# Four seven-product couples in both mixers' output projections, their weight sums made ahead by way of HBM, and an affine step moved from VectorE to ScalarE

## The chip, the cores and the metric

The kernel runs on one core of a Trainium2 chip. The metric is the device time of one execution in microseconds (us). TensorE (PE) multiplies matrices, VectorE (DVE) and ScalarE (ACT) do element-wise work, GpSimd (POOL) some more of it, and SyncE (SP) issues most of the DMA transfers between HBM and the on-chip memory.

## The reference

An encoder trunk of two layers over one sequence of 256 tokens, model width 2048. Layer 0 has a bidirectional mLSTM mixer (8 heads), layer 1 a bidirectional HGRN2 mixer (16 heads); each is followed by a ConvGLU feed-forward network (FFN, 5504 wide).

```python
def mlstm_mixer(hn, w_in, b_gate, head_g, w_out):
    p = hn @ w_in
    ...
    y = head_rmsnorm(y, head_g, A_HEADS) * jax.nn.sigmoid(o)
    return y @ w_out

def hgrn_mixer(hn, w_in, lb, head_g, w_out):
    p = hn @ w_in
    ...
    def gate(f):
        log_f = jnp.logaddexp(log_lb, log_1mlb + jax.nn.log_sigmoid(f))
        k = (1.0 - lb) * jax.nn.sigmoid(-f)
    ...
    y = head_rmsnorm(y, head_g, B_HEADS) * jax.nn.silu(g)
    return y @ w_out
```

`y @ w_out` is the output projection that the change is about, a product of 256 x 2048 by 2048 x 2048. The gate is, without logarithms, `g = lb + (1 - lb) * sigmoid(f)`: the affine step of the change.

## The kernel before, in words

Products are made in float32 precision out of three products of reduced ones: each operand is split into a high part (`wh`, a cast on ScalarE at L144) and a low part (`wl`, a subtract on VectorE at L145), both in `parts`. Raw weights come in tiles `raw` of 128 x 2048 (1 MB), three in rotation, loaded in order on SP's queue (`load_raw`, L132). So every weight passes through a DMA, ScalarE and VectorE before TensorE reads it.

A projection is a list of chunks, each of 512 output columns and both halves of 128 tokens. In `mixed`, which makes both mixers' output projections, column block 0 is an ordinary chunk (`c0`, matmuls at L356), columns 512 to 1535 are a couple (`two`, made by `pair`, matmuls at L231), and column block 3 is again an ordinary chunk (`c3`). A couple has 8 units, each of two 128-row blocks of the weights: a 2 x 2 product of blocks that takes eight products, each of three matmuls of 128 x 512. For the units listed in `SEVEN_MIX`, (2, 4, 6), a scheme with seven products is used instead (`squares_by_seven`): it needs sums of four token blocks (`token`, `token_sums`: tile f at L635 and L540, then the split sums sx at L541 and L542) and sums of the weights' blocks.

In the mixers' couples the weights' sums are made in place by `combine` (L203): four VectorE subtracts of 128 x 512 for each unit, into a tile T and into raw itself. The FFNs' couples do it otherwise: their sums were made ahead. `prepare` loads the unit's raw weights into two tiles praw (on SP's queue, through `late` at L378), makes the sums by four subtracts (L603), and stores them in HBM (`tscr`, L606); the couple then loads T (768 KB, L194) and the last quarter of raw (256 KB, L195) from `tscr`. `prepare` is a side job with a period that sets how often a unit is made; the first eight units of each layer's FFN are prepared in the mixer before it (`prepare_early`, called with a first time and a period: 45.0 and 19.0 in layer 0, 30.0 and 26.0 in layer 1), the others in the FFN.

T and the token-sum tile f have the same tag "avc" (`temporary`): three buffers in the FFN's pool "ff", two in the pool "op" of a mixer's couple. This pool is opened when c0 is done in program order and lies over the memory of the mixer's own pool, so its first tiles wait for the last readers of the mixer's tiles, among them the last transposes pz (L1087 in layer 1).

The order of instructions on each engine is made by a scheduler that models their times; loads on SP's queue wait there in order until the buffer that they write is free.

In `hgrn`, each head and direction makes the gate: Sigmoid of z on ScalarE (L978), Sigmoid of −z (L979), then the affine step on VectorE (L980), and GpSimd's product with q (L981), from which the chunked recurrence goes on.

Of the kernel before, what the change touches and what calls it, by code (L numbers as in the profile page):

```python
# [49 lines left out]
SEVEN = (1, 2, 3, 4, 6, 7, 8, 9), (1, 2, 4, 5, 7, 8)  # L50
SEVEN_END = (1, 2, 3, 4, 5, 6, 7)
END = 3
SCRATCH = 4096
SEVEN_MIX = (2, 4, 6)

# [7 lines left out]
def trunk_kernel(ctx, tc, xT, x_d, fg_d, pp_d, cst_d, w_gate, w_first, w_aq, w_ak, w_av, w_ao, w_aout, w_ao2,  # L63
                 w_bq, w_bv, w_bg, w_bout, w_bo2, w_up, w_d0, w_d1, w_d2, w_d3, out, mscr, tscr):
    nc = tc.nc
# [61 lines left out]
    pin = tc.keep_in_program_order  # L127
    turns = dict(w=0)

# [488 lines left out]

    def mixed(w, w2, x, norm, close):

        c0, _, _, c3 = project(lambda c: w[c // 3], KT, x, norm)
        op, SX, first = ExitStack(), {}, c0.done

        def sums(u):
            side.until(lambda: u in SX)
            return SX[u]

        two = pair(w2, KT, 1, x, sums, norm, SEVEN_MIX)

        def token():  # L630
            for i, u in enumerate(SEVEN_MIX):
                f = temporary(two.pool, "f")
                for j in range(2):
                    y = x(2 * u + j).bitcast(F32)
                    dve.tensor_tensor(f[:, j * T:(j + 1) * T], y[:, 0:T], y[:, T:2 * T], ALU.add)  # L635
# [12 lines left out]
        return [c0, two, c3]  # L648


    def mlstm(norm, nxt):
# [192 lines left out]
        for pr in range(AH // 2):  # L844
# [36 lines left out]
            def done_first(ps, done_v=done_v):  # L881
# [10 lines left out]
                side.push(start(gs))  # L892
                prepare_early(box["mp"], 0, 45.0, 19.0)

# [30 lines left out]

        return chunks + mixed(w_aout, w_ao2, yx, nxt, stack.close)


    def hgrn(norm, nxt):
# [4 lines left out]
        def begin():  # L934
            mp = box["mp"] = stack.enter_context(tc.tile_pool(name="hg", bufs=1))
            late(cst[:, C_LV:], cst_d[:, C_LV:])
            prepare_early(mp, 1, 30.0, 26.0)
            box["turn"] = 0
# [23 lines left out]
        def take(hd, what, ps):  # L962
# [16 lines left out]
            act.activation(kz, z, AF.Sigmoid, scale=-1.0)  # L979
            dve.tensor_scalar(g, g, oml[:, hd:hd + 1], lb[:, hd:hd + 1], ALU.mult, ALU.add)  # L980
            pool.tensor_tensor(QZ[:, (1 - dr) * T:(2 - dr) * T], st["q"], g, ALU.mult)  # L981
# [143 lines left out]

        return chunks + mixed(w_bout, w_bo2, yx, nxt, stack.close)


    def ffn(layer, norm, nxt):
        stack = ExitStack()  # L1130
        ending = isinstance(nxt, FinalNorm)
        seven = SEVEN[0], SEVEN_END if ending else SEVEN[1]
        box = dict(n=(2 * len(SEVEN[0]) + len(SEVEN[1])) * layer)
        chunks, pairs = [], []
# [41 lines left out]
        for part, (f0, nf) in enumerate(((0, FA), (FA, FB))):  # L1176
# [137 lines left out]
def build(nc, ins, out_shape=(2, P, D), **kw):  # L1314
# [3 lines left out]
    mscr = nc.dram_tensor("mscr", (64, T), F32, kind="Internal").ap()  # L1318
    tscr = nc.dram_tensor("tscr", (4 * len(SEVEN[0]) + len(SEVEN[1]) + 2 * len(SEVEN_END), P, 2048), F32, kind="Internal").ap()
    with tile.TileContext(nc, schedule_with_timeline_sim=True) as tc:  # L1320
# [17 lines left out]
```

## Time and profile before

| | us |
|---|---|
| median of 3 runs (2383.26 to 2383.58) | 2383.42 |
| profiled execution | 2384.87 |
| its span in the trace | 2382.9 |

| stretch of the profiled execution | from, us | to, us |
|---|---|---|
| layer 0's mixer up to its couple | 10 | 326 |
| layer 0's couple (a) | 326 | 368 |
| layer 1's mixer up to its couple | 1080 | 1577 |
| layer 1's output columns 0 to 511 | 1577 | 1608.4 |
| layer 1's couple (b) | 1608.4 | 1656.1 |

The profile gives for each engine how long it was busy, for each line of the kernel the number, busy time and mean duration of its instructions and the idle time before them with what ended it ("idle before <-releaser"). The chain of waits follows the work that ended last back from the end, and lists in order of time what the end depended on. A view by windows gives busy times, the granted TensorE clock (PEclk, 1.00 is full speed) and DMA traffic for a stretch. Matmuls follow each other faster than the duration shown for one, because they are pipelined; their pace is the distance of starts. Names are those of the program's tiles: `wl<-raw,wh` reads raw and wh and writes wl.

### The profile page before, as it was taken

How to read it: one execution, taken by the hardware profiler on the slowest of the kernel's cores; microseconds unless marked ns; L12 is line 12 of the kernel's file. 1: busy time of each engine (PE TensorE's matmuls, PEld its weight loads, DVE VectorE, ACT ScalarE, POOL GpSimd, SP SyncE). 2: the span in 40 equal slices, each digit the busy share in tenths (PEclk: the TensorE clock that was granted, in tenths of full speed). 3: DMA queues.
4: the chain of work that ended last, by engine and by line, in shares of the span. 5: the costliest groups of instructions: out<-in, count | busy, mean ns of one | idle time of the engine just before them, and what ended most of it. 6: DMA issues, size and time to landing. Idle time of an engine off the chain costs nothing.

```text
span 2382.9 us, 38182 instructions
## 1 busy us (share of the span) xinstructions
PE 2365.6 (99%) x14572; PEld 2024.3 (85%) x14572; DVE 1938.4 (81%) x3001; ACT 1433.6 (60%) x2271; POOL 205.4 (9%) x242
## 2 busy tenths in 40 slices
PE   9999999999999999999999999999999999999998
PEld 7888888888888888888888888887888888888886
DVE  7777687888788887766888888888788788888787
ACT  7655456555665555655666666665555566455565
POOL 0100000000000000001233222320000000000000
PEclk9999999999999999999999999999999999999999
DMA  8777656886697885755666666764788588887695
GB/s 300 240 272 268 227 174 214 302 303 226 223 354 272 283 280 195 274 190 204 244 234 228 246 236 227 245 225 173 258 299 283 195 309 310 288 288 253 204 345 201
DMA packets 112471, 601.23 MB, mean 252 GB/s; under 512 B 12688, under 2 KB 13200, under 8 KB 66464
## 3 DMA queue, kind: packets, MB, share of 16 engines
q1 hardware_dynamic: 110592, 594.78, 71.1%
q0 software_dynamic: 1120, 3.21, 0.8%
q8 instruction: 114, 1.87, 0.3%
q10 hardware_dynamic: 576, 0.79, 0.1%
q14 instruction: 69, 0.57, 0.1%
HBM read 542.05 MB, written 56.69 MB: 251 GB/s over the span
## 4 chain that ended last, share of the span: by engine, by line
PE 95%; DVE 2%; DMA 1%; issue 1%; ACT 0%; SPq 0%; POOL 0%; DVEq 0%; POOLq 0%; ACTq 0%
PE mm L340 36%; PE mm L356 18%; PE mm L344 18%; PE pc L231 12%; PE mm L231 6%; DMA praw<-in_w_d 1%; PE py L1066 1%; PE pn L808 1%; DVE wl L145 1%; PE pd L1016 0%; PE pz L417 0%; PE pa L1016 0%; DVE QK L1029 0%; DMA Mb<-mscr 0%; DMA raw<-in_w_first 0%
## 5 line engine op out<-in xcount | busy, mean ns | idle before, releaser
L340 PE MATMUL mm<-xt,wh 128*128 128x512 f32 x3776 | 1314.2, 394 | 0.0
L145 DVE TENSOR_TENSOR wl<-raw,wh 128x1024 fp32r<-128x1024 f32 (+1 forms) x845 | 1034.6, 1229 | 274.6 <-ACT wh L144 268.9
L144 ACT CAST wh<-raw 128x1024 fp32r<-128x1024 f32 (+1 forms) x845 | 875.6, 1042 | 520.4 <-PE mm L340 293.6
L344 PE MATMUL mm<-xt,wl 128*128 128x256 f32 x3776 | 1046.3, 278 | 0.0
L340 PEld LDWEIGHTS mm<-xt,wh 128*128 128x128 f32 x3776 | 706.2, 188 | 160.1
L344 PEld LDWEIGHTS mm<-xt,wl 128*128 128x128 f32 x3776 | 709.7, 188 | 4.5 <-issue 0.4
L356 PE MATMUL mm<-wh,xt 128*128 128x512 f32 x1024 | 320.5, 391 | 2.2 <-ACT xt L362 1.6
L231 PE MATMUL pc<-wh,g 128*128 128x512 f32 x676 | 228.0, 389 | 0.0
L356 PEld LDWEIGHTS mm<-wh,xt 128*128 128x128 f32 x1024 | 191.1, 188 | 41.8 <-ACT xt L362 2.0
L356 PE MATMUL mm<-wl,xt 128*128 128x512 f32 x512 | 197.9, 391 | 0.0
L603 DVE TENSOR_TENSOR praw<-praw 128x512 f32<-128x512 f32 x208 | 143.8, 691 | 49.4 <-DMA praw<-in_w_d 39.0
L231 PEld LDWEIGHTS pc<-wh,g 128*128 128x128 f32 x676 | 126.9, 188 | 26.4
L231 PE MATMUL pc<-wl,g 128*128 128x512 f32 x338 | 131.5, 389 | 0.0
L145 DVE TENSOR_TENSOR wl<-T,wh 128x1024 fp32r<-128x1024 f32 (+1 forms) x116 | 110.2, 961 | 20.2 <-ACT wh L144 19.5
L231 PE MATMUL mm<-wh,sx 128*128 128x512 f32 x348 | 124.4, 391 | 0.0
L144 ACT CAST wh<-T 128x1024 fp32r<-128x1024 f32 (+1 forms) x116 | 96.2, 836 | 45.8 <-PE pc L231 20.3
L564 POOL TENSOR_TENSOR hm<-hm,u 128x512 f32<-128x512 f32 x9 | 12.6, 1395 | 1186.4 <-DVE u L563 592.3
L1029 DVE TENSOR_TENSOR QK<-QK,G 128x256 f32<-128x256 f32 x224 | 109.7, 537 | 5.4 <-ACT kq L1008 5.0
L356 PEld LDWEIGHTS mm<-wl,xt 128*128 128x128 f32 x512 | 96.2, 188 | 19.1
L1150 ACT COPY avc<-mm 128x256 f32<-128x256 f32 x172 | 64.2, 373 | 78.2 <-PE mm L344 78.2
L1008 ACT COPY kq<-QK 128x512 f32<-128x512 f32 x112 | 74.5, 669 | 57.3 <-DVE QK L1029 44.6
L1151 DVE TENSOR_TENSOR avc<-mm,avc 128x256 f32<-128x256 f32 x172 | 71.9, 418 | 12.7 <-ACT avc L1150 12.6
(247 smaller groups left out, 2322.3 us busy)
## 6 DMA issues: line engine op xcount, KB each, us to landing
raw<-in_w_up SPq DMA_DIRECT2D x172, 1024.0 KB, 5.4
praw<-in_w_d SPq DMA_DIRECT2D x104, 512.0 KB, 6.8
tscr<-praw SPq DMA_DIRECT2D x104, 512.0 KB, 6.8
raw<-in_w_bq SPq DMA_DIRECT2D x48, 1024.0 KB, 5.0
raw<-in_w_d SPq DMA_DIRECT2D x52, 768.0 KB, 6.1
T<-tscr SPq DMA_DIRECT2D x52, 768.0 KB, 7.7
raw<-in_w_d SPq DMA_DIRECT2D x32, 1024.0 KB, 5.2
raw<-in_w_ao SPq DMA_DIRECT2D x24, 1024.0 KB, 4.9
```

Source lines behind the costliest of these rows:

```text
L144: pin(act.copy(wh[:, :m], r))
L145: pin(dve.tensor_tensor(wl[:, :m], r, wh[:, :m].bitcast(F32), ALU.subtract))
L231: pe.matmul(ps, a, b, start=id(ps) not in begun, stop=stop and i == 2)
L340: pe.matmul(ps[f], wh[:, c:c + P], x, start=k + kk == 0, stop=False)
L344: pe.matmul(ps[f][:, 0:T], wl[:, c:c + P], x[:, 0:T], start=False, stop=k + kk == ch.nk - 1)
L356: pe.matmul(ps[t], x[:, a + t * P:a + (t + 1) * P], w[:, c], start=st and i == 0, stop=sp and i == 2)
L603: dve.tensor_tensor(out, x, y, ALU.subtract)
L808: pe.matmul(pn[:, 0:258], w, v, start=(i == 0), stop=(i == len(parts) - 1))
L1008: act.copy(m, blocks(QK, h))
L1029: dve.tensor_tensor(two[:, j], two[:, j], by[:, j], ALU.mult)
L1150: act.copy(z, p[:, T:2 * T])
L1151: dve.tensor_tensor(z, p[:, 0:T], z, ALU.add)
```

## The change

Both couples of the mixers now have four units with seven products, `SEVEN_MIX = (2, 3, 5, 6)`. The weights' sums of these units are no longer made in the couple: like the FFNs' they are put ahead of the list that `prepare_early` works off in the mixer, so each mixer prepares 12 units, 4 for its own couple and 8 for the FFN behind it; the periods are shortened from 19.0 to 13.0 and from 26.0 to 16.0. The couple loads T and the quarter of raw from `tscr` (L194, L195). `tscr` has eight more slots, and a helper `store` gives out slots for mixers and FFNs. `combine` is still there and is no longer called. T and f still share two buffers in the couple's pool.

The forget gate's affine step becomes an Identity activation with bias and scale on ScalarE, behind the second Sigmoid.

```diff
-SEVEN_MIX = (2, 4, 6)
+SEVEN_MIX = (2, 3, 5, 6)
...
+    def store(ch, src, u, todo):
+        ch.stored[u] = tscr[turns["t"]]
+        turns["t"] += 1
+        todo.append((src[:, 2048 * u:2048 * (u + 1)], ch.stored[u]))
+
-    def mixed(w, w2, x, norm, close):
+    def mixed(w, w2, x, norm, close, layer):
...
         two = pair(w2, KT, 1, x, sums, norm, SEVEN_MIX)
+        for u in SEVEN_MIX:
+            store(two, w2, u, early[layer][0])
+        two.waits = early[layer][1]
...
-                prepare_early(box["mp"], 0, 45.0, 19.0)
+                prepare_early(box["mp"], 0, 45.0, 13.0)
...
-        return chunks + mixed(w_aout, w_ao2, yx, nxt, stack.close)
+        return chunks + mixed(w_aout, w_ao2, yx, nxt, stack.close, 0)
...
-            prepare_early(mp, 1, 30.0, 26.0)
+            prepare_early(mp, 1, 30.0, 16.0)
...
-            dve.tensor_scalar(g, g, oml[:, hd:hd + 1], lb[:, hd:hd + 1], ALU.mult, ALU.add)
+            act.activation(g, g, AF.Identity, bias=lb[:, hd:hd + 1], scale=oml[:, hd:hd + 1])
...
-        return chunks + mixed(w_bout, w_bo2, yx, nxt, stack.close)
+        return chunks + mixed(w_bout, w_bo2, yx, nxt, stack.close, 1)
...
-                    ch.stored[u] = tscr[box["n"]]
-                    todo.append((src[:, 2048 * u:2048 * (u + 1)], tscr[box["n"]]))
-                    box["n"] += 1
+                    store(ch, src, u, todo)
```

More of the change, by code (lines that the diff above doesn't have):

```diff
@@ L127, in trunk_kernel @@
     pin = tc.keep_in_program_order
-    turns = dict(w=0)
+    turns = dict(w=0, t=0)
     def load_raw(src, b0, b1, start=nc.sync.dma_start):
@@ L1132, in ffn @@
         seven = SEVEN[0], SEVEN_END if ending else SEVEN[1]
-        box = dict(n=(2 * len(SEVEN[0]) + len(SEVEN[1])) * layer)
+        box = {}
         chunks, pairs = [], []
@@ L1318, in build @@
     mscr = nc.dram_tensor("mscr", (64, T), F32, kind="Internal").ap()
-    tscr = nc.dram_tensor("tscr", (4 * len(SEVEN[0]) + len(SEVEN[1]) + 2 * len(SEVEN_END), P, 2048), F32, kind="Internal").ap()
+    tscr = nc.dram_tensor("tscr", (2 * len(SEVEN_MIX) + 4 * len(SEVEN[0]) + len(SEVEN[1]) + 2 * len(SEVEN_END), P, 2048), F32, kind="Internal").ap()
     with tile.TileContext(nc, schedule_with_timeline_sim=True) as tc:
```

## The prediction

> **What bounds the kernel now.** I read the page's busy shares and chain first, then the stretches of the span around the places that the change touches.
>
> ```profile
> PE 2365.6 (99%) x14572; PEld 2024.3 (85%) x14572; DVE 1938.4 (81%) x3001; ACT 1433.6 (60%) x2271; POOL 205.4 (9%) x242
> PE 95%; DVE 2%; DMA 1%; issue 1%; ACT 0%; SPq 0%; POOL 0%; DVEq 0%; POOLq 0%; ACTq 0%
> ```
>
> TensorE is busy 99% of a span of 2382.9 us, and the chain is TensorE's for 95%. So only two things can pay: fewer matmuls, and the few microseconds in which TensorE waits. The view by windows has both mixers and both couples (one mixer's output columns 512 to 1535):
>
> ```profile
> core 0: us, PE busy (x) PEld busy (x) DVE busy (x) ACT busy (x) POOL busy (x), PEclk, DMA share, GB/s
> 10.00:326.00 316.00, 314.98 (x1630) 266.08 (x1631) 238.01 (x439) 188.21 (x315) 20.25 (x31) 1.00 0.73 253
> 326.00:368.00 42.00, 42.00 (x187) 34.79 (x186) 40.18 (x58) 25.15 (x31) 0.00 (x0) 1.00 0.56 195
> 1080.00:1577.00 497.00, 496.09 (x4462) 427.75 (x4461) 419.15 (x712) 333.31 (x620) 147.08 (x175) 1.00 0.67 236
> 1608.40:1656.10 47.70, 45.79 (x191) 36.32 (x191) 42.91 (x65) 24.48 (x31) 0.00 (x0) 0.96 0.48 169
> ```
>
> Layer 0's couple (a) runs without a gap, though VectorE is busy for 40.18 of its 42 us. Layer 1's couple (b) holds the same work and takes 47.7. The chain of waits gives the pace, and its rows in b give the cause:
>
> ```profile
> 326.27 10.88 PE pc L231 x48
> 1612.05 0.12 PE pz L1087
> 1619.83 1.14 DVE wl L145
> 1629.73 0.63 ACT sx L541
> 1630.38 0.76 DVE sx L542 x2
> 1631.59 1.29 DVE T L203 x2
> 1632.88 0.61 DVE raw L203
> 1634.52 1.05 ACT wh L144
> ```
>
> 48 matmuls in 10.88 us are 0.2267 us each. A couple has 183 at L231, so 41.5 us; in b five matmuls of the first quarter fall in between, 1.1 more, so b would take 42.7 us and loses about 5.0. Its mixer ends later against the couple: the last transposes (pz) come at 1612.05, after the couple has begun, and VectorE is behind from there: splits, token sums (f, sx), then the weights' sums (T, raw, L203) one after another, with TensorE at their end:
>
> ```profile
> 1634.67 0.50 PE L231 MATMUL pc<-wh,yb 128*128 128x512 f32 x1 [1.56 <-ACT wh L144]
> 1635.62 1.22 PE L231 MATMUL pc<-wh,yb 128*128 128x512 f32 x2 [0.21 <-ACT wh L144]
> 1632.60:1635.60 3.00, 1.24 (x5) 0.38 (x3) 3.00 (x6) 2.03 (x3) 0.00 (x0) 1.00 0.01 3
> 1635.60:1639.00 3.40, 3.38 (x8) 2.55 (x9) 3.40 (x5) 2.85 (x4) 0.00 (x0) 0.50 0.31 51
> ```
>
> The first two are TensorE's waits, the others windows. Right after the wait the granted clock is 0.50 for 3.4 us: 8 matmuls where 15 fit, about 1.6 us lost. So the 5.0 are 1.6 of clock and some 3.4 of waiting.
>
> **The change, part by part.**
>
> *One more seven-product unit a couple.* Three matmuls of 0.2267 less: −0.68 us each, −1.36 together, if nothing waits.
>
> *The weights' sums leave the couple.*
>
> ```profile
> L203 DVE TENSOR_TENSOR T<-raw x12: 680/683/693, 323.1 to 1634.6; 128x512 f32<-128x512 f32 x12
> L203 DVE TENSOR_TENSOR raw<-raw x6: 680/682/683, 324.4 to 1633.4; 128x512 f32<-128x512 f32 x6
> L203 DVE TENSOR_TENSOR T<-raw,T x6: 679/683/683, 329.7 to 1636.9; 128x512 f32<-128x512 f32 x6
> L145 DVE TENSOR_TENSOR wl<-T,wh 128x512 fp32r<-128x512 f32 x3 | 2.0, 682 | 0.0
> L540 DVE TENSOR_TENSOR f<-f 128x128 f32<-128x128 f32 x12 | 2.8, 283 | 0.0
> L635 DVE TENSOR_TENSOR f<-yb 128x256 f32<-128x256 f32 x6 | 2.2, 417 | 0.0
> L542 DVE TENSOR_TENSOR sx<-f,sx 128x512 fp32r<-128x512 f32 x3 | 2.0, 686 | 0.5 <-ACT sx L541 0.5
> ```
>
> Twelve subtracts a couple go. Back to back they start 0.60 apart (two of them 1.29 above): −7.2 us of VectorE. The fourth unit adds two splits (1.14 + 0.60) and one token sum (2 × 0.34 + 4 × 0.20 + 0.60 = 2.1; starts lie 0.08 closer than the durations): +3.8. Net −3.4 us a couple.
>
> *What comes in their place is a load.* T now comes from tscr, and T shares a tag of two buffers with the token-sum tile f in this pool (three in the FFNs). In the changed kernel's order unit 2's T takes one, its f the other, the f of units 3 and 5 follow, and unit 3's T is issued only when an f has been read by its last sx: in a that of unit 5, in b that of unit 3. So unit 3's weights stand behind a row of VectorE work, a transfer and a cast. Loads of this kind land as follows (last line of the view of T, two FFN windows, and a raw load in couple b):
>
> ```profile
> DMA to landing us min/median/max: 4.1/7.7/10.0
> 637.00:766.00 129.00, 129.00 (x599) 107.73 (x598) 107.17 (x119) 79.43 (x93) 7.48 (x4) 1.00 0.83 305
> 1677.00:1926.00 249.00, 249.00 (x1436) 217.66 (x1436) 205.28 (x330) 140.59 (x222) 0.70 (x1) 1.00 0.75 259
> raw<-in_w_bo SPq DMA_DIRECT2D x4, 1024.0 KB, 4.8
> ```
>
> The median comes from the FFNs, where more is in flight (259 to 305 GB/s, the windows' last column, against 169 to 195 in the couples above), so I take 4.8, with 4.1 and 7.7 as ends.
>
> Couple b.
>
> ```profile
> L144 ACT CAST wh<-T 128x512 fp32r<-128x512 f32 x3 | 1.9, 618 | 0.6 <-DVE T L203 0.6
> L509 ACT ACTIVATE jk<-hm 128x512 f32<-128x512 f32 x2 | 1.3, 628 | 0.6 <-DVE hm L523 0.6
> L523 DVE TENSOR_TENSOR hm<-hm,mm 128x512 f32<-128x512 f32 x2 | 1.4, 679 | 0.0
> ```
>
> T of unit 2 is issued after pz, 1612.1, and lands at 1617; VectorE's queue ahead (f and L540 1.5, the last yb 0.4, two splits 2.3, sums into hm 1.2, from 1612.2) ends at 1617.6 too. ScalarE is in order: behind T's first cast (0.62) stands a Square for the norm (0.63), then T's long cast (1.05), so VectorE has it at about 1619.2, after 1.6 us with one 0.6 split. Then up to unit 3's sx: five long splits 5.7, one sx 0.6, four f 1.34, eight L540 1.64, ScalarE's sx 0.63, VectorE's sx 0.69: 10.6 us. Unit 3's T is issued at 1629.8, lands at 1634.6, is cast at 1635.7. TensorE's first need is 1608.4 + 0.1 + 1.1 + (24 + 24 + 21 + 6) × 0.2267 = 1626.6 at full pace; the order puts products of units 3 to 5 ahead of it, until some 1633. From the cast 90 matmuls are left, 20.4 us, and about 0.45 waits for the low part: end 1656.5, against 1656.1 before. If the clock falls again (a gap of some 2.7 us, more than the 1.56 above) 1.6 more: **b +2.0 us**. Ends: landing in 4.1 without the drop −0.3, 7.7 with it +4.9.
>
> On the drop: here it followed a wait of 1.56 us. [...]
>
> Couple a. VectorE after the sums into hm (from 327.2): 1.2 for these, four long splits 4.6, two sx with ScalarE's 1.9, f and L540 1.8: unit 3's T is issued at about 336.7. TensorE needs it at 326.3 + (48 + 21 + 6) × 0.2267 = 343.3. Landing in 4.8, and some tenths more for the megabyte queued just ahead of it, gives a cast at 342.6 to 343.3: just in time, **a −0.3**. Ends: −0.7; with 7.7, a cast at 345.5, 2.2 + 0.45 of waiting and a clock drop of 1.6, +3.6.
>
> *The preparation moves into the mixers.*
>
> ```profile
> L603 DVE TENSOR_TENSOR praw<-praw 128x512 f32<-128x512 f32 x208 | 143.8, 691 | 49.4 <-DMA praw<-in_w_d 39.0 <-issue 9.8
> praw<-in_w_d SPq DMA_DIRECT2D x104, 512.0 KB, 6.8
> tscr<-praw SPq DMA_DIRECT2D x104, 512.0 KB, 6.8
> ```
>
> Each mixer prepares 12 units, not 8, with period 13 instead of 19 and 16 instead of 26. Four units are 16 subtracts at L603, 16 × 0.69 = 11 us of VectorE, and 8 MB of DMA, on SP's queue among the weight loads; a praw load waits there for the landing of the store from the same buffer, 6.8 us, and the weight loads queued behind wait too. VectorE waits for praw in its queue, at the rate above 49.4/208 × 16 = 3.8 us a mixer. Mixer a has VectorE at 75%, TensorE's gaps are 1.0 us in 316, and weights are loaded up to three tiles ahead, which hides all of this if no wait exceeds that reserve. I take +0.3, with −0.9 (all gaps of b gone) and +3 as ends; without the cover four units cost 4 × 6.8 = 27 us on SP.
>
> *The affine step.*
>
> ```profile
> L980 DVE TENSOR_SCALAR G<-G,oml,lb 128x256 f32<-128x256 f32 x32 | 15.7, 492 | 0.5 <-ACT G L978 0.5
> L1155 ACT ACTIVATE avc<-avc,pp 128x256 f32<-128x256 f32 x86 | 51.5, 599 | 45.5 <-DVE avc L1153 45.2
> L981 POOL TENSOR_TENSOR QK<-q,G 128x256 f32<-128x256 f32 x32 | 37.9, 1184 | 148.2 <-DVE G L980 123.2 <-PE mm L340 12.5 <-PE mm L344 12.4
> ```
>
> VectorE loses 15.7 us of its 419 in mixer b (more than the 11 that preparation adds), ScalarE gains 32 × 0.6 = 19.2 on 333, 67% to 71%. It has the same Identity form with bias and scale at L1155; the built program loads as many tables as before. G comes after the second sigmoid instead of beside it, about half a us later per head and direction; POOL, at 30%, passes that on to a head whose products lie behind many others. TensorE idles 0.9 us in this mixer, so the step is worth nothing that counts: 0.
>
> **Sum.** −0.3 + 2.0 + 0.3 = +2.0 us on the profiled execution's 2384.87 (1.45 above the median), so 2386.9 there and 2385.4 on the median of 2383.42.
>
> **Rivals.**
> 1. *The relief holds.* VectorE has 3.4 us less to do in b, and T arrives before TensorE has run out: no wait, no clock drop. b −5.0 − 0.7, a −0.7: −6.4, 2377.0. For it: VectorE alone is behind the present gap. Against: T's place behind the token sums puts it later than the subtracts stood. 0.17.
> 2. *Landing decides (slower).* With T at the group's median of 7.7, b is +4.9 and a +3.6, mixers 0.3: +8.8, 2392.2. From about 6.5 us on (a 0.7, b 3.7) the change is slower by over 0.2%. [...] 0.21.
> 3. *SP's queue in the mixers (slower).* A weight load queued behind a praw load that waits for a store comes later than the three tiles in reserve last: 1 to 2 us in four to six of the 24 units, +7: 2390. Against: eight units a mixer already run so, with gaps of 1 us. 0.13.
> 4. [...] This is inside the forecast's side, 0.15 of it.
>
> **How the numbers follow.** Forecast with rival 4: 0.49. About 0.2%, 4.8 us, is what a measurement of this kernel tells from no change. Faster 0.17, same 0.49, slower 0.34. Likeliest case alone 2382 to 2388; the range takes in most of rivals 2 and 3 and reaches towards rival 1: 2378 to 2395.
>
> **What would show it.** L203 gone; in couple b a TensorE gap near 1633 released by the cast of T, and its T issued after a token sum's sx, landing in about 4.8; PEclk 0.5 behind it; couple a near 41.7 us; mixers unchanged within 1 us. Wrong, if T in b lands before 1631, if a stalls by more than 1 us, or if gaps appear in the mixers.

## The result and the profile after

The changed kernel is slower: 2411.07 us, median of 4 runs (2409.57 to 2412.63), against 2383.34 us for the kernel before (4 runs on the same chip, 2382.31 to 2383.58). The ratio is 1.0115, with a 95% interval from 1.0102 to 1.0129. The profiled execution took 2412.63 us, with a span of 2410.9. The forecast of 2385.4 was wrong, and the time lies above the range. From the page after, busy shares and chain:

```profile
PE 2377.5 (99%) x14566; PEld 2026.5 (84%) x14566; DVE 1936.7 (80%) x2995; ACT 1448.1 (60%) x2309; POOL 203.5 (8%) x242
PE 86%; DMA 6%; DVE 4%; issue 3%; ACT 1%; POOL 1%; SPq 0%; DVEq 0%; POOLq 0%; ACTq 0%
```

Six matmuls fewer, and yet TensorE is busy 11.9 us longer. The chain was TensorE's for 95%; now it is for 86%, with 6% for transfers and 3% for issue. The same view by windows as before, with the couples' windows moved to where they lie now, and a window in the middle of each layer's mixer and of layer 0's FFN:

```profile
core 0: us, PE busy (x) PEld busy (x) DVE busy (x) ACT busy (x) POOL busy (x), PEclk, DMA share, GB/s
10.00:330.00 320.00, 317.19 (x1631) 265.88 (x1632) 248.38 (x462) 187.98 (x317) 21.28 (x31) 1.00 0.79 277
330.00:375.40 45.40, 42.86 (x181) 34.70 (x180) 34.83 (x49) 24.86 (x31) 0.00 (x0) 0.96 0.67 239
450.00:600.00 150.00, 150.00 (x851) 129.99 (x850) 126.50 (x206) 82.50 (x132) 0.00 (x0) 1.00 0.78 266
1092.00:1600.00 508.00, 498.75 (x4439) 428.32 (x4440) 416.94 (x698) 346.95 (x649) 145.18 (x175) 1.00 0.71 250
1631.60:1684.10 52.50, 46.45 (x191) 35.35 (x189) 38.37 (x60) 26.98 (x35) 0.00 (x0) 0.97 0.58 208
```

The mixers have gaps of 2.8 and 9.3 us, both couples have gaps of 2.5 and 6 us and a clock below 1, and layer 0's FFN has no gap at all but 851 matmuls in 150 us. The kernel before has 867 there:

```profile
450.00:600.00 150.00, 150.00 (x867) 131.19 (x866) 126.46 (x208) 84.14 (x135) 0.00 (x0) 1.00 0.78 272
```

The lengths of the stages, each from one mark in the trace to the next (the first product of layer 0's gate projection, then the first and the last matmul of each couple at L231), are the yardstick for all that follows:

| kernel | mixer a | couple a | FFN a | mixer b | couple b | FFN b, first part | span |
|---|---|---|---|---|---|---|---|
| before | 296.1 | 41.25 | 270.3 | 575.8 | 47.6 | 270.3 | 2382.9 |
| after | 300.0 | 45.23 | 274.7 | 587.0 | 52.3 | 270.2 | 2410.9 |
| difference | +3.9 | +4.0 | +4.3 | +11.2 | +4.7 | −0.2 | +28.0 |

FFN a is the first part of layer 0's FFN, 22 chunks. The second parts of both FFNs and the end are the same within 0.1 us. So 28 us have five places, each with its own cause to be found. Each kernel has one profiled execution, and the lengths are of that one; other executions of the same kernel can differ by several us (2400.07 to 2407.31 us with four buffers, 2386.35 to 2397.25 with the affine step alone). A wait of TensorE is given below as the time between two starts beyond their usual spacing; that is some 0.17 us more than the timeline's idle time in brackets, which counts from the end of a matmul (one at L231 is shown 0.39 us long, with starts 0.2267 apart).

### The profile page after: what moved, and what is told of

Its sections match the earlier page's. It is cut to its first block, busy times and chain, and to the rows that moved or that the text cites. A ratio compares the mean times of both kernels' runs of the same rounds, so it can differ in the third digit from the quotient of the medians.

```text
span 2410.9 us, 38276 instructions
## 1 busy us (share of the span) xinstructions
PE 2377.5 (99%) x14566; PEld 2026.5 (84%) x14566; DVE 1936.7 (80%) x2995; ACT 1448.1 (60%) x2309; POOL 203.5 (8%) x242
## 4 chain that ended last, share of the span: by engine, by line
PE 86%; DMA 6%; DVE 4%; issue 3%; ACT 1%; POOL 1%; SPq 0%; DVEq 0%; POOLq 0%; ACTq 0%
PE mm L340 35%; PE mm L344 17%; PE mm L356 14%; PE pc L231 11%; PE mm L231 6%; DMA praw<-in_w_d 2%; DVE wl L145 1%; DMA T<-tscr 1%; DMA praw<-in_w_ao 1%; DMA tscr<-praw 1%; ACT wh L144 1%; DVE praw L603 1%; PE py L1074 1%; DVE QK L1037 1%; POOL QK L989 0%
## 5 line engine op out<-in xcount | busy, mean ns | idle before, releaser
L340 PE MATMUL mm<-xt,wh 128*128 128x512 f32 x3776 | 1317.9, 395 | 1.7 <-issue 1.7
L344 PE MATMUL mm<-xt,wl 128*128 128x256 f32 x3776 | 1049.3, 279 | 1.1 <-issue 1.0
L340 PEld LDWEIGHTS mm<-xt,wh 128*128 128x128 f32 x3776 | 706.5, 188 | 163.0 <-issue 1.2
L344 PEld LDWEIGHTS mm<-xt,wl 128*128 128x128 f32 x3776 | 710.4, 188 | 6.7 <-issue 2.2
L356 PE MATMUL mm<-wh,xt 128*128 128x512 f32 x1024 | 322.4, 393 | 1.5 <-ACT xt L362 1.3
L231 PE MATMUL pc<-wh,g 128*128 128x512 f32 x676 | 227.9, 389 | 0.0
L356 PEld LDWEIGHTS mm<-wh,xt 128*128 128x128 f32 x1024 | 191.9, 188 | 41.9 <-ACT xt L362 1.7
L603 DVE TENSOR_TENSOR praw<-praw 128x512 f32<-128x512 f32 x240 | 168.1, 700 | 73.1 <-DMA praw<-in_w_d 45.7
L356 PE MATMUL mm<-wl,xt 128*128 128x512 f32 x512 | 198.3, 391 | 0.2 <-issue 0.2
L231 PEld LDWEIGHTS pc<-wh,g 128*128 128x128 f32 x676 | 126.9, 188 | 26.6
L231 PE MATMUL mm<-wh,sx 128*128 128x512 f32 x360 | 130.4, 395 | 6.8 <-ACT wh L144 6.8
L231 PE MATMUL pc<-wl,g 128*128 128x512 f32 x338 | 131.4, 389 | 0.0
L356 PEld LDWEIGHTS mm<-wl,xt 128*128 128x128 f32 x512 | 96.6, 189 | 19.4 <-DVE wl L145 0.3
L1037 DVE TENSOR_TENSOR QK<-QK,G 128x256 f32<-128x256 f32 x224 | 103.5, 512 | 9.0 <-ACT kq L1016 8.9
L231 PEld LDWEIGHTS mm<-wh,sx 128*128 128x128 f32 x360 | 68.3, 190 | 22.3 <-ACT wh L144 8.5
```

The costliest lines, as they stand in the source:

```text
L231: pe.matmul(ps, a, b, start=id(ps) not in begun, stop=stop and i == 2)
L340: pe.matmul(ps[f], wh[:, c:c + P], x, start=k + kk == 0, stop=False)
L344: pe.matmul(ps[f][:, 0:T], wl[:, c:c + P], x[:, 0:T], start=False, stop=k + kk == ch.nk - 1)
L356: pe.matmul(ps[t], x[:, a + t * P:a + (t + 1) * P], w[:, c], start=st and i == 0, stop=sp and i == 2)
L603: dve.tensor_tensor(out, x, y, ALU.subtract)
L1037: dve.tensor_tensor(two[:, j], two[:, j], by[:, j], ALU.mult)
```

## The experiments

The theories after the result: the couples wait for T behind the token sums (the forecast's mechanism); the mixers lose by the preparation, either by its amount (more units) or by its rate; or they lose by the affine step, through the gates; and the FFN's loss is a second pace that something ahead of it selects.

**The couples.** The chain of the kernel after in couple a (start us, us, what) and in couple b:

```profile
338.99 1.36 SPq L195
340.44 7.82 DMA T<-tscr
349.29 1.05 ACT wh L144
350.39 0.79 PE pc L231
```

```profile
1651.87 0.70 DVE sx L542
1652.59 4.42 DMA T<-tscr
1657.04 1.05 ACT wh L144
1662.21 0.61 DVE sx L542
1662.84 11.30 DMA T<-tscr
1674.17 1.05 ACT wh L144
```

Each T is issued when the last sx has read an f (in a the third sx, unit 5's, ends at 340.16, and T is issued at 340.44), lands, and is cast, and a matmul waits at the end. With four buffers in place of two, unit 3's T waits for unit 2's token sums alone:

```diff
-        return pool_.tile([P, 1536], F32, tag="avc", bufs=TEMP if pool_.name == "ff" else 2, name=name)
+        return pool_.tile([P, 1536], F32, tag="avc", bufs=TEMP if pool_.name == "ff" else 4, name=name)
```

> The changed kernel with four buffers instead of two for T and the token sums f in the mixers' couples; unit 3's T then waits in both couples for unit 2's token sums alone. Theory C (the couples lose by T standing behind the sums of unit 3 and 5): couple a back from 45.2 to 40.6 us, couple b from 52.3 to 43 to 46, the clock drops in the couples gone; 10 to 14 us less, 2397 to 2401. Rival D (the loads themselves collide, landing in 7.8 to 11.3 us with several in flight): the wait moves to the landing of T for unit 2 or 6, and less than 4 us come back.

Measured 2402.85 us, 1.0074 [1.0057, 1.0091]. Its windows over the two couples:

```profile
331.60:372.40 40.80, 40.80 (x181) 33.80 (x180) 32.99 (x41) 24.05 (x29) 0.00 (x0) 1.00 0.76 272
1637.00:1683.00 46.00, 44.10 (x186) 35.61 (x185) 42.16 (x64) 27.75 (x35) 3.29 (x2) 0.96 0.69 251
```

Couple a has no gap and full clock, and its length is 40.58 us: 0.67 under before, three matmuls of 0.2267. The buffer is the whole loss in a. Couple b falls from 52.3 to 46.4, 1.2 under before. VectorE is busy 42.2 of its 46 us, and the one wait over 1 us (1.57, ended by a split wl) has a clock drop behind it; that VectorE is what keeps b from 42 is read from this and was not tried. The mixers stay as slow as after, or slower (303.0 and 590.3).

The other way to the same products is to make the sums in the couple, as before, with four units:

```diff
-SEVEN_MIX = (2, 4, 6)
+SEVEN_MIX = (2, 3, 5, 6)
```

> The kernel before with four seven-product units a couple, their weights' sums still made in the couple by VectorE (4 subtracts more a unit). By the prices of the prediction VectorE has 2.4 + 3.8 = 6.2 us more in each couple, for 0.68 us less of matmuls; it was busy for 40.2 of couple a's 42 us, so a becomes VectorE's: a +2 to +5, b +2 to +6, 2388 to 2394, all else as before. If TensorE still sets the couples: 2382.

2399.66 us, 1.0065 [1.0049, 1.008]. Couple a takes 51.9 us, b 49.9. In a, 26 matmuls of the columns behind it (L356) run inside these 51.9 us, 5.9 us at 0.2267, so the couple itself takes some 46.0, 4.7 more than before. VectorE decides there:

```profile
324.70:376.70 52.00, 49.29 (x207) 39.37 (x206) 50.17 (x76) 28.35 (x35) 3.03 (x2) 0.97 0.54 187
```

VectorE is busy 50.2 of 52 us. So a fourth unit cannot simply be added; the stored sums do relieve VectorE (34.8 us in the row of after). Its mixers are as before (296.2 and 575.6). The rest of its loss, and the reason why it lies above what was expected, is the pace of the first parts of both FFNs (353.3 ns for a pair of matmuls in place of 346.7, see below): FFN b's first part takes 274.7 us; FFN a takes 268.8, but without the 5.9 us that ran in the couple.

With the old periods in the changed kernel:

```diff
-                prepare_early(box["mp"], 0, 45.0, 13.0)
+                prepare_early(box["mp"], 0, 45.0, 19.0)
...
-            prepare_early(mp, 1, 30.0, 16.0)
+            prepare_early(mp, 1, 30.0, 26.0)
```

> The changed kernel with the old periods, 19 and 26, and still 12 units a mixer (12 x 19 + 45 = 273 of 316 us, 12 x 26 + 30 = 342 of 497 us, so they fit). Theory A in its strict form (it is the period): both mixers back to within 2 us of before, 13 us less, some 2398. Theory A in its weak form (it is the number of units): no more than 4 us less, 2407. Theory B: layer 0's mixer gains up to 3, layer 1's nothing, 2408.

2454.29 us, 1.0292 [1.0277, 1.0308]: the couples take 67.9 and 79.6 us. TensorE's waits in couple a, then its window:

```profile
PE pc L231 <- ACT sx L541: 16.0, 1, 16.0
```

```profile
324.80:393.00 68.20, 47.53 (x182) 37.46 (x181) 44.67 (x68) 26.08 (x33) 0.00 (x0) 0.80 0.60 214
```

The couple's `two.waits` is the whole list of the mixer, 12 units in layer 0 and 19 in layer 1 (the text ahead of the result and the forecast say 12 units for each mixer, and 8 before; layer 1 had 15 before). What the schedule hasn't reached is done in one burst at the couple. So the change needs its shorter periods; and with the old one mixer a is 295.7 us, as before, though it makes ten units in place of eight.

**The preparation's rate.** The kernel before, with 8 units in layer 0's mixer and 15 in layer 1's, with the new periods alone:

```diff
-                prepare_early(box["mp"], 0, 45.0, 19.0)
+                prepare_early(box["mp"], 0, 45.0, 13.0)
...
-            prepare_early(mp, 1, 30.0, 26.0)
+            prepare_early(mp, 1, 30.0, 16.0)
```

> The kernel before with the short periods (13, 16) and nothing else: 8 units in layer 0's mixer and 15 in layer 1's, as before, made faster one after another. If the rate is what costs (VectorE stands at praw because load, subtracts and store take longer than the period): layer 0's mixer +2 to +4, layer 1's +2 to +6, 2388 to 2393. If the number of units costs: within 1.5 us of before in both. The FFNs and couples as before.

2391.70 us, 1.0031 [1.0018, 1.0044]. Mixer a takes 299.1 us, 3.1 more, with no unit added. In all ten profiled kernels with the old period mixer a takes 295.7 to 296.2 us, in all eight with the new one 297.5 to 303.0. In mixer a it is the rate, not the amount. VectorE's idle time before the subtracts on praw in mixer a (60 to 325 us: total, times, longest), in the kernel before and in the kernel after:

```profile
DVE praw L603 <- DMA praw<-in_w_d: 6.7, 5, 2.5
```

```profile
DVE praw L603 <- DMA praw<-in_w_d: 19.2, 7, 4.5
DVE praw L603 <- issue: 8.1, 2, 5.2
DVE praw L603 <- DMA praw<-in_w_ao: 6.4, 3, 3.9
```

That is 6.7 us before, 33.7 after, and 21.7 with the new periods alone. What stands behind these subtracts in VectorE's queue comes late, and TensorE loses its time in many waits, none of them over 0.9 us in these two kernels. SP's waits in the same stretch in the kernel before, after, and in the one with the new periods alone:

```profile
SPq L378 <- DMA tscr<-praw: 0.4, 1, 0.4
```

```profile
SPq L378 <- DMA tscr<-praw: 32.6, 15, 5.1
```

```profile
SPq L378 <- DMA tscr<-praw: 17.7, 6, 5.5
```

SP's weight loads and praw loads are one queue, and it now stands up to 5 us at a time before the landing of a store. The weight loads themselves are in time: ScalarE's cast waits 0.2 us in all for loads of raw in mixer a after, and not at all in mixer b. The chain of the kernel after shows why the queue cannot keep the period:

```profile
92.58 7.24 DMA tscr<-praw
99.83 4.85 DMA praw<-in_w_ao
...
108.98 7.05 DMA tscr<-praw
116.05 5.96 DMA praw<-in_w_ao
...
126.19 7.31 DMA tscr<-praw
133.52 6.02 DMA praw<-in_w_ao
```

A praw pair is loaded, subtracted, stored, and loaded again: a ring of some 17 us (92.58 to 108.98 to 126.19). A period of 13 planned us asks for more than that, so the ring never rests. The units are 19.0 us apart in mixer a, after and with the new periods alone; before they were 25.6 apart, and the ring had 8 us of slack. Two pairs might break the ring; that was not tried.

Mixer b is another matter. With the new periods alone it takes 579.1 us, 3.3 more, but SP waits there only 1.1 us for the landing of a store (1.3 after), and TensorE's one wait over 0.25 us is not behind the preparation: it is a wait of 3.37 us marked issue, where the kernel before has one of 0.91. What such waits are, the affine step shows below.

Is it the bytes loaded? In the next kernel every unit but the first of a list loads 64 columns of each tile's 1024, into one fixed pair of tiles; the sums of these units are not those of the weights, the subtracts and stores stay:

```diff
-                    start(r[j], todo[i][0][:, j * 1024:(j + 1) * 1024])
+                    n = 64 if short and i else 1024
+                    start(r[j][:, 0:n], todo[i][0][:, j * 1024:j * 1024 + n])
```

> The changed kernel with one fixed pair praw, whose loads after the first unit's bring 64 of 1024 columns (so the sums of all later units are not those of the weights); subtracts, stores and their waits stay. Theory A (VectorE waits in order for praw's landing): layer 0's mixer back from +3.8 to +1 or less, and in layer 1's the waits of 0.7 to 1.7 us behind praw gone, about -5. Theory F (several of TensorE's longest waits in layer 1's mixer end 1.4 us after a 16 KB fetch of its instructions, late behind much DMA traffic): those waits of 1.1 to 2.1 us and the clock drop behind them go too, about -5 more, 2397 in all. If VectorE's own work is the cause: less than 3 us less, 2408.

2405.39 us, 1.0089 [1.0072, 1.0106]. Mixer a 298.4 us, so 1.6 of the 3.9 come back; mixer b 582.6, so 4.4 of 11.2. The loads are a part; the stores and subtracts at the same rate keep 2.3 us in mixer a. In mixer b no wait marked issue of 0.25 us or more is left, nor a clock drop; the waits over 0.25 us that stay, 4.7 us in all, are for products of VectorE and ScalarE.

**The affine step.** Alone in the kernel before (behind the second Sigmoid), alone and in the source ahead of the second Sigmoid, and undone in the kernel after, by itself and with the four buffers:

```diff
-            dve.tensor_scalar(g, g, oml[:, hd:hd + 1], lb[:, hd:hd + 1], ALU.mult, ALU.add)
+            act.activation(g, g, AF.Identity, bias=lb[:, hd:hd + 1], scale=oml[:, hd:hd + 1])
```

> The kernel before with nothing but the affine step moved to ScalarE. Theory A: within 2 us of before, 2383. Theory B: layer 1's mixer 8 to 11 us longer, some 2393, all else as before.

2387.97 us, 1.0021 [1.0012, 1.003]; mixer b 581.7, all other stages as before.

```diff
             act.activation(g, z, AF.Sigmoid)
+            act.activation(g, g, AF.Identity, bias=lb[:, hd:hd + 1], scale=oml[:, hd:hd + 1])
             act.activation(kz, z, AF.Sigmoid, scale=-1.0)
-            dve.tensor_scalar(g, g, oml[:, hd:hd + 1], lb[:, hd:hd + 1], ALU.mult, ALU.add)
```

> The kernel before with the affine step on ScalarE, this time ahead of the second Sigmoid, so that G is ready some 0.3 us earlier than with the step behind it. Theory B (the gate's chain: G later, POOL and the recurrence wait): layer 1's mixer +4 to +6, somewhat less than with the step behind. Theory F (the step as such costs nothing; the order of instructions shifts, and TensorE meets its instruction fetch at another point): any value from -1 to +6, with every TensorE wait over 1 us in that mixer ending some 1.4 us after the last packet of a 16 KB instruction fetch, and none ended by a product of the gate.

2389.11 us, 1.002 [1.0011, 1.0029]; mixer b 579.9. The scheduler put the step behind the second Sigmoid all the same: on each engine the instructions of the two kernels are the same in the same order. So this is the program of the kernel with the affine step alone once more. It says nothing of the step's place, and shows how far mixer b varies between executions: 581.7 and 579.9.

```diff
-            act.activation(g, g, AF.Identity, bias=lb[:, hd:hd + 1], scale=oml[:, hd:hd + 1])
+            dve.tensor_scalar(g, g, oml[:, hd:hd + 1], lb[:, hd:hd + 1], ALU.mult, ALU.add)
```

> The changed kernel with the affine step back on VectorE. The changed kernel is 27.7 us slower, of which the distances of the couples' first matmuls put 11.2 in layer 1's mixer, 3.8 in layer 0's, 4.0 and 4.7 in couples a and b, 4.3 in layer 0's FFN. Theory A (preparation ring: a unit's load, four subtracts and store take some 17 to 20 us one after another in one pair of buffers, and a period of 13 or 16 asks for more, so VectorE waits in order for praw): no change beyond 2 us, some 2410. Theory B (the gate's chain on ScalarE is late and POOL, then the recurrence, wait): the 11 us of layer 1's mixer go, some 2400, the rest stays.

2404.27 us, 1.0085 [1.007, 1.01]; mixer b 581.4. The couples are shorter too, 42.9 and 50.6 (after: 45.2 and 52.3).

The kernel with this line and `bufs=4`, as in the four-buffer kernel above:

> The changed kernel with both of the earlier edits, affine on VectorE and four buffers. If the parts add up: couples at 40.6 and 46.4 or less, layer 1's mixer +5.5 instead of +11.2, layer 0's mixer +5, its FFN +4.3: some +13 to +14 against before, 2397. If they share one cause, more than 2400 or less than 2394.

2394.95 us, 1.0045 [1.003, 1.006]; mixer b 580.8, couples 40.6 and 45.0.

In mixer b the affine step on ScalarE costs 4.1 to 5.9 us alone, the new rate 3.3 alone and 4.9 to 5.5 with the added units, both together 11.2 to 15.3 (four kernels). With the affine step, the old periods and the added units it is 8.3, of which two waits just ahead of the couple are 3.0. That is not through a late gate: in the traces the affine step ends 0.80 us (median) after the end of the first Sigmoid when it is on ScalarE, and 1.48 us after it on VectorE before. G comes earlier, not later, and no TensorE wait over 0.25 us in mixer b is released by the gates' product on POOL. TensorE's long waits are of another kind. Its timeline in the kernel with the affine step alone:

```profile
1333.07 0.89 PE L1016 MATMUL pd<-kq 128*32 128x32 f32 x76
1336.27 0.25 PE L1016 MATMUL pd<-kq 128*32 128x32 f32 x2 [2.31 <-issue]
1336.44 1.16 PE L356 MATMUL mm<-wh,xt 128*128 128x512 f32 x2
```

"issue" says that TensorE waited for nothing that the profile shows. The DMA view of the stretch 1333.5 to 1334.8 has the queue that carries instructions, beside the data (packets, MB, share of the 16 engines):

```profile
q1 hardware_dynamic: 41, 0.31, 91.5%
q8 instruction: 1, 0.02, 5.6%
```

One packet of 16 KB runs from 1333.6 to 1334.75, while the data holds the engines at 91.5%, and TensorE goes on 1.5 us after it. Over the whole span of after the page has

```profile
q8 instruction: 114, 1.87, 0.3%
```

and 29,132 instructions on TensorE (14566 matmuls and as many weight loads): 255.5 a packet. In the trace after, 13 packets go with 3263 TensorE instructions from 10 to 330 us, 251 each, and 34 with 8879 from 1092 to 1600 us, 261 each, while one comes every 24.6 us in the first stretch and every 14.9 in the second, for 35.5 and 20.5 instructions of VectorE and 24.4 and 19.1 of ScalarE. The packets keep step with TensorE's instructions alone, so this queue is read as the one that brings TensorE's own program. In a stretch of tiny matmuls, 76 with their loads in 0.89 us, such a packet's 255.5 are used up in about 1.5 us (an estimate from these numbers). No run here changed the fetches themselves, so this link is read from the times: in all profiles, every wait over 0.7 us that is marked issue in mixer b ends 1.2 to 1.5 us after the end of such a packet (0.91 us in the kernel before; 0.94, 1.77 and 2.50 with the affine step alone; 1.36 and 2.09 in its second run; 3.37 with the new periods alone; 2.13, 1.11 and 1.81 after). With the affine step alone these waits are together 4.3 us more than before, in the second run 2.5, and each run has a clock drop behind the longest; mixer b is 5.9 and 4.1 us longer. So fetch waits, with the clock, are about all that the step costs. Why one fetch comes late and another does not is not shown. It may go with the data in flight: with the short praw loads (215 GB/s from 1092 to 1600 us, 250 after) no such wait is left.

So mixer b's 11.2 us: in the trace after, fetch waits of 2.13 + 1.11 + 1.81 less 0.91 of before, and 1.6 of clock behind the first, 5.7. Four others, 1.12 + 0.73 + 1.56 + 1.65 = 5.1, are released by a product of VectorE, or of ScalarE behind VectorE, that stands in VectorE's queue behind praw; a last one of 0.47 is marked issue. The chain to the one of 1.56:

```profile
1417.44 8.58 DMA praw<-in_w_d
...
1431.02 0.69 DVE praw L603
1431.70 0.68 DVE QK L1037 x2
...
1432.52 0.46 PE pa L1048 x2
```

A praw load that lands late holds up VectorE's queue, then its last subtract and QK come one after the other, and TensorE at their end. This is VectorE's wait of which the forecast said 3.8 us a mixer without a place where it would be felt. But it takes both edits: with the affine step back on VectorE only the wait at QK is left of the four (0.8 and 0.9 us), with the affine step alone none. Why the two together cost more than their sum was not tried.

**Layer 1 alone, and the FFN's pace.** In the FFN a product of two matmuls (L340 and L344) takes 346.7 ns before and 353.3 ns after, through the whole of FFN a, without waits and at full clock. The next kernels try what selects it. Three tiny matmuls as disturbances in layer 0's FFN:

```diff
+            def bump():
+                d = aux("idle")
+                pe.matmul(d[0:QUAD, 0:53], ones[:, 0:QUAD], ones[:, 0:53], start=True, stop=True)
...
-                                    prep if i == 0 else None,
+                                    prep if i == 0 else bump if not layer and not part and i in (4, 10, 16) else None,
```

> The changed kernel with three tiny extra matmuls (32 x 53) among the products of layer 0's FFN, before the 5th, 11th and 17th of its 22 first chunks. That stage takes 4.3 us more than before without one wait above 0.35 us: a pair of matmuls (L340, L344) takes 353.3 ns instead of 346.7 from its first to its last chunk. If this is a rhythm that persists once fallen into: the pace changes to 346.7 at one of the bumps, 2 to 3.5 us less, 2408. If it is set by something lasting (addresses, traffic): it stays at 353.3, 2411.

2417.65 us, 1.0141 [1.0126, 1.0156]: FFN a 275.9, the slow pace kept through all three. Here FFN b's first part is slow as well (274.3), and mixer b takes 590.1.

One tiny matmul into a tile of mm ahead of FFN a, which turns the order of the PSUM tiles by one:

```diff
+                for _ in range(1 if layer == 0 and not part else 0):
+                    d = psm.tile([P, 512], F32, tag="mm", name="mm")
+                    pe.matmul(d[0:QUAD, 0:53], ones[:, 0:QUAD], ones[:, 0:53], start=True, stop=True)
```

> The changed kernel with one tiny matmul into a tile of the tag mm ahead of layer 0's FFN, which changes the order of PSUM banks there from 3,0,2,1 to 0,3,2,1 and in layer 1's FFN from 3,2,1,0 to 0,2,1,3. If the order of banks sets the pace: layer 0's FFN at 346.7 ns a pair, 4.3 less, and layer 1's at 353.3, 4 to 5 more. If it is chance or something else: no link with these orders, both stages as in the changed kernel (353.3 and 346.7).

2410.40 us, 1.0108 [1.0095, 1.0122]: FFN a is 270.7, the fast pace, as the order of banks would have it; but FFN b's first part, which should then have turned slow, stays at 270.2. The kernels below speak against the order too.

A version that keeps what the runs had shown to be good, against the kernel before: only layer 1's couple has four stored units, T has two buffers of its own and f one, periods and affine step are as before, and four of the list's units go to the FFN's parts, so that mixer b prepares 15:

```diff
-SEVEN_MIX = (2, 4, 6)
+SEVEN_MIXES = (2, 4, 6), (2, 3, 5, 6)
...
+        if pool_.name == "op1":
+            return pool_.tile([P, 1536], F32, tag=name, bufs={"T": 2, "f": FB1}[name], name=name)
...
-                chunks.append(two(w_d3, 2, None, seven[1], *early[layer]))
+                chunks.append(two(w_d3, 2, None, seven[1], *early[layer], some=3))
```

> What the runs so far point to: layer 0, the affine step, the periods (19, 26) and the number of units in each mixer (8, 15) as before; only layer 1's couple has four units with sums made ahead, its T has two buffers of its own and f one, and four units of the last FFN couple, whose place they take in the mixer, are prepared in the FFN instead (two more in each part). If the couples' loss was the shared buffers and the mixers' loss the rate: couple b 42 to 44 instead of 47.6, all else within 1 us of before, 2378 to 2380. If rate does not matter but the stores as such, or if the FFN's preparation is now too fast: 2383 to 2390.

2388.57 us (11 runs, 2384.67 to 2389.92), 1.0017 [1.0008, 1.0026]. Couple b takes 43.8 us, 3.7 less than before, without a clock drop:

```profile
1606.50:1650.40 43.90, 43.59 (x189) 34.48 (x188) 36.40 (x58) 24.49 (x33) 0.00 (x0) 1.00 0.68 252
```

Mixers a and b are as before. But FFN b's first part now takes 275.4 us at the slow pace, 5.1 more, and its second part 4.5 more. With a tiny matmul into mm behind couple b, as had helped in layer 0:

```diff
-        c0.done, c3.before = done, op.close
+        def after_two():
+            op.close()
+            for _ in range(1 * layer):
+                d = psm.tile([P, 512], F32, tag="mm", name="mm")
+                pe.matmul(d[0:QUAD, 0:53], ones[:, 0:QUAD], ones[:, 0:53], start=True, stop=True)
+
+        c0.done, c3.before = done, after_two
```

> The layer-1-only kernel with one tiny matmul into a tile mm behind couple b, which changes the order of banks in layer 1's FFN from 3,2,0,1 to 3,2,1,0 (its weight tiles stay where they are). If the order of banks sets the pace: that stage back to 270.3 us, 5 less, 2383 to 2384. If not: as without the matmul, 2388.6.

2387.90 us, 1.0015 [1.0006, 1.0024]: FFN b 274.9, the slow pace, in an order of PSUM tiles that the turn had made the good one. Its windows before and behind one wait of 0.79 us at 1850:

```profile
1760.00:1840.00 80.00, 80.00 (x455) 69.35 (x454) 67.51 (x110) 42.07 (x68) 0.00 (x0) 1.00 0.83 289
1860.00:1920.00 60.00, 60.00 (x349) 52.91 (x347) 51.73 (x84) 37.05 (x60) 0.00 (x0) 1.00 0.66 223
```

5.69 matmuls a microsecond, then 5.82. The pace flips at a wait, back again at another (2171.5 us), and holds between. The order of the PSUM tiles is not what selects it.

The same with 16 units in the mixer and period 24 (`prepare_early(mp, 1, 30.0, 24.0)`, `some=4`):

> The same, with one of the two extra units of the FFN's second part moved back to the mixer (16 units there, period 24 instead of 26). In the layer-1-only kernel this second part had two waits of about 1 us behind praw and the slow pace behind them, 4.5 us in all. If its faster preparation was the cause: that stage back to within 1 us of before, couple b still at 43.8 instead of 47.6, 2379 to 2380, below both kernels. If the pace is set by chance: 2379 to 2389.

2390.60 us, 1.0025 [1.0016, 1.0035]: mixer b 581.6, with two fetch waits of 1.56 and 1.21 us and two waits for products of VectorE of 1.45 and 0.82, FFN b's first part slow (275.4), its second as before.

Last, is it the FFN's own preparation, which has four units more here? Two and four units of the last couple are left out of the seven-product list (`seven[1][:5]`, and `seven[1][:3]` with the preparation as before). In both, the dropped units' ordinary products read a token block that token sums have overwritten, so their values are not the reference's; the number of products is as said.

> The layer-1-only kernel, whose last FFN couple has five seven-product units instead of seven (2 x 0.68 us more of matmuls); two units stay in the FFN's first part, none is added to the second. If the pace comes with the extra units of the first part: that part +5, second part as before, couple b -3.7: 2386. If it comes by chance: 2381 or 2386.

2385.95 us, 1.0009 [0.9999, 1.0018].

> The same with three instead of seven units in the last FFN couple (4 x 0.68 = 2.7 us more) and the FFN's preparation exactly as before. If the pace came with the extra preparation: layer 1's FFN at 346.7 ns, couple b -3.7, last couple +2.7, 2382 to 2383, at or just below before. If it comes with the stored couple ahead of the FFN: that stage still +5, 2387.

2387.15 us, 1.0013 [1.0004, 1.0021]. Both have FFN b's first part at 275.4 and couple b at 43.7 to 43.8. With the preparation as before the pace is slow all the same, so that is not the cause either. All five kernels with this couple b have the slow pace behind it. Over all 18 profiles the first part of an FFN is slow only behind a couple with four seven-product units (15 of 23 such places; the kernel with the sums made in the couples has it in both layers), and never behind one with three (none of 13). What in the longer list does it, and why not always, stays open. No kernel that was run beat the kernel before: the nearest, within 0.2% of it, is the one with two units dropped.

## Why the prediction was wrong

*The step that failed* is "The preparation moves into the mixers", "which hides all of this if no wait exceeds that reserve. I take +0.3, with −0.9 (all gaps of b gone) and +3 as ends". Measured: +3.9 in a, and in b +4.9 to +5.5 with the affine step undone (+11.2 with it). The step counted units, 11 us of VectorE and 8 MB, and it held eight units a mixer for proof that units are hidden. In mixer a the kernel with eight units and the new periods shows that they are not: what counts is the rate, against a ring of load, subtract, store of some 17 us in one pair of buffers. The term for VectorE's wait before praw, 3.8 us a mixer, was 27 us there. In mixer b, where 19 units are made and not 12, the loss of 11.2 us is, in the trace after, 5.7 of waits read as waits for instructions and of the clock behind one, a term that the step did not have, and 5.1 behind praw, seen only with the affine step; rate and amount were not separated there. Rival 3, at +7 and a chance of 0.13, had SP's queue behind the stores, but not the way: the weight loads were never late, VectorE was. The words "eight units a mixer already run so" spoke against it and should not have: in mixer a they ran at a unit in 25.6 us. The forecast had both numbers, 6.8 us for each transfer and 13 for the period.

*The affine step*, "worth nothing that counts: 0", costs 4 to 6 us by itself, while its durations were right (32 × 592 ns = 18.9 us against 19.2). The step had G half a microsecond later and asked who waits for it. G came 0.7 us earlier, nobody waits for it, and the cost is in TensorE's waits marked issue (4.3 and 2.5 us more in the two runs), read above as waits for its instructions, for which the step had no term.

*The couples* had the right mechanism and the wrong size: +1.7 forecast, +8.7 measured; rival 2 said +8.5. The T of unit 3 was issued 10.5 us after the start of couple a (10.4 forecast) and 21.0 after that of b (21.7), behind the sx named. In a the landing was mis-sized: 7.82 us, not 4.8, with a megabyte of weights and a quarter of raw issued in the 2 us ahead of it and another T 4.5 us behind; the wait is 2.48 us, with the clock drop of the upper end. In b unit 3's T landed in 4.42, in the forecast's range, but the T of unit 6 took 11.30 with four loads in flight, above every value that the group had shown, and cost 2.75 us more. The clock drop was priced at 1.6 us in b; the program with the affine step alone has couple b at 47.0 us in the execution without the drop and at 47.7 in the one with it, so there it is worth 0.75. The forecast took "4.8" from loads in a couple that had few in flight; the change itself puts more there (239 GB/s against 195 in a).

*The FFN* stood at nothing, and no step named it: +4.3. Its cause stays open.

*What was right:* L203 is gone; a unit is worth 0.68 us (0.67 with four buffers); the clock falls to half behind gaps of the size seen before, for some 3.4 us (3.413 at each of three places in the trace after); VectorE is relieved in the couples.

On the clock, the 0.15 of rival 4 had no run behind it, and after the change the clock did not stay up: the trace after has the drop behind 2.48 us (couple a), 2.13 us (mixer b, at 1224.1) and at a wait of 1.57 us (couple b, at 1657.6). The windows around the second, with a clock of 0.53 in the middle one:

```profile
1220.00:1224.00 4.00, 2.06 (x58) 1.69 (x49) 1.88 (x6) 1.98 (x7) 0.00 (x0) 1.00 0.94 315
1224.00:1227.60 3.60, 3.60 (x11) 2.79 (x10) 2.52 (x7) 2.91 (x7) 0.00 (x0) 0.53 0.97 386
1227.60:1231.00 3.40, 3.40 (x20) 2.88 (x19) 2.62 (x6) 2.83 (x4) 0.00 (x0) 1.00 0.32 129
```

## What to carry to other kernels

Work that is "hidden" has a rate as well as an amount: ahead of moving work under an engine, add up the round trip of one buffer (load, work, store, and the next load's wait), and compare it with the period at which it is wanted (here some 17 us against 13). A load that is issued when a shared buffer comes free is priced by what is queued then, by the change itself too (here 7.82 and 11.30 us to landing, where the forecast took 4.8); two more buffers took the whole loss of couple a away. In a stretch of many tiny matmuls like mixer b, the five kernels with the affine step or the new rate, but not both, lost 3.3 to 5.9 us, so a forecast of zero for a harmless move there deserves a range of plus 6. And an edit that is meant to move an instruction has to be looked up in the trace: the scheduler may have put it back.

## What the hardware showed that was not expected

- TensorE waits for its own program, as far as the times show it: its waits of over 0.7 us marked issue in mixer b end 1.2 to 1.5 us after a packet of 16 KB on the queue of instructions. One such wait, 3.37 us, in the kernel before with the new periods, on TensorE's timeline (the longest of all runs, 4.41 us, is in the kernel with three tiny matmuls, at 1243.6):

```profile
1238.38 0.39 PE L344 MATMUL mm<-xt,wl 128*128 128x256 f32 x1 [3.21 <-issue]
```

- The clock did not fall behind that wait of 3.37 us, nor behind waits of 1.81 (after, 1373.9) and 1.77 us (affine step alone, 1231), though it fell behind 1.72 (before), 1.85, 2.13, 2.48 and 2.50. In these traces length alone does not decide. Around the wait of 3.37 us the clock is 1.00:

```profile
1230.00:1245.00 15.00, 11.79 (x191) 10.25 (x190) 9.87 (x21) 7.78 (x18) 1.66 (x3) 1.00 0.80 261
```

  Apart from the one at the end of each run, a drop is recorded as 3.413 us long or a multiple of it, and the drops within one trace start whole multiples of that apart: after, at 350.25, 1224.06 and 1657.55, which is 256 and 127 of them. Laid out on a grid of 3.413 us through the drops of its trace, the wait of 3.37 us (idle from 1235.17 to 1238.38) is cut in two at 1236.6, 1.45 and 1.76 us, while the one of 2.48 us (idle from 347.12 to 349.44) lies whole between 346.84 and 350.25. In all profiles, leaving out the first 15 us and the end, each stretch of the grid with 1.95 us or more of TensorE idle has a drop right behind it (16 stretches at full clock), none with 1.0 to 1.46 us has (21), and between the two there are both. So in these traces 1.95 us of one stretch idle, a little over half, was enough, and the gap of 3.37 us, which a border cuts, passed. No run here moved a gap on purpose.
- Two paces of the same matmul pairs, 346.7 and 353.3 ns (1.9%), each held for hundreds of microseconds at full clock and without waits, changed by a wait of a microsecond. Disturbance by tiny matmuls, the order of the PSUM tiles and the FFN's own preparation were tried and do not select it; the slow pace was seen in first parts behind couples with four units alone. What selects it stays open; here it was worth 4 to 5 us in each FFN part, as much as couple b could gain.
